# Six places for projection weights, latents scaled ahead of the low-half search, and sliding attention's keys ahead of its values

## The chip, the cores and the metric

The kernel runs on one core of a Trainium2 chip. The time is the device time of one execution in microseconds (us); shown is the median of several runs. A profile comes from one execution of its own. The engines are called as in the profile: PE (TensorE, matrix multiplications and transposes), PEld (its weight loads), DVE (VectorE), ACT (ScalarE), POOL (GpSimd) and SP (SyncE, which issues most DMAs). Each engine works through its own queue in order, and waits at an instruction whose inputs or target are not free.

## The reference

One decoder block over 1024 tokens and 16 learned meta tokens, all in float32:

```python
hn = rms_norm(h, attn_norm_g)
proj = hn @ w_in
aq, ak, av, bq, bkv, iq, ik, iw, gates = jnp.split(proj, IN_SPLITS, axis=-1)
o_a = sliding_window_sink_attention(aq, ak, av, sinks, bias_a)      # window 128, 8 heads, 2 key heads
q = (rms_norm(bq, q_norm_g) @ w_uq).reshape(b, p, 8, 64)
c_kv = rms_norm(bkv, kv_norm_g)                                     # latent keys/values, 128 wide
o_b = indexed_sparse_mla(q_abs, c_kv, iq, ik, iw, w_uv, bias_b)     # each query attends to its 256 best keys
mixed = sig(gA) * (o_a @ w_branch_a) + sig(gB) * (o_b @ w_branch_b)
h = h + mixed @ w_out
h = h + (silu(rms_norm(h) @ w_ffn_gate) * (rms_norm(h) @ w_ffn_up)) @ w_ffn_down
```

The 256 best keys of a query come from an index score, `sum over 4 heads of relu(iq . ik) * iw`; of equal scores the earlier keys count.

## The kernel before

The tokens lie in eight blocks of 128, and the meta tokens in a ninth of 16. Every float32 product is made of three: an operand is split into a high part (a copy rounded to `float32r`, made by ACT) and a low part (the difference, made by POOL or DVE), and `mm3` (L193 issues its matmuls) adds high x high, high x low and low x high. So each weight tile passes through a raw place filled by a DMA, a copy on ACT (L187, `wa_hi`) and a subtraction on POOL (L188, `wa_lo`).

`phase1` does, in this order of the program text:

- `load_x`, `setup`, `norm_x`: load the tokens, normalise and transpose them (`xt`, `xh`).
- `indexer`: the index projections and scores (`scores[j]`, for the blocks 1 to 7; block j has 144 + 128 j columns). The upper 16 bits of each score are kept as `high[j]`.
- `select_topk`: finds each row's 256th largest score bit by bit, first in the upper 16 bits, then in the lower ("low halves"). There are three searches side by side. `search_dve` handles the blocks 6, 4 and 1: in each of 16 steps DVE counts, for each block, the scores above a threshold (L815) and moves the threshold with three small operations (L819, L820; L832 to L834 in the low halves). `search_act` handles the blocks 7 and 2 in one group, 5 and 3 in another: ACT counts with a sign function and an accumulator (L857), and POOL moves the threshold (L865 once for each block of the group, then L866). Between the halves `low_halves` extracts the lower 16 bits (L801 on POOL) and blanks those whose upper half differs (L802 on DVE). Then DVE makes each block's mask: counts, equal scores, a running sum over them (L781 to L791), and POOL scales it (L792) and cuts it to the causal part (L538).
- `proj_tokens`: two projections of 256 columns each for all blocks. The first (`part` 0) gives the query latents. The second gives the 128 columns of the key latents and the 128 of sliding attention's values, which go to DRAM (L569). Squares are summed by ACT (L565); from them DVE makes `rlat`, the scale of every row.
- `window_inputs`: keys and queries of sliding attention, by feature, stored to DRAM (`wk_dram`, `wq_dram`).
- `latents`: DVE scales the latents (L586, `lraw`), PE transposes them (L198, tile `tp`), ACT and DVE split them into `qn` and `ck`.
- `sparse_inputs`: queries, keys and values of the sparse attention from the latents, stored to DRAM.
- `window_setup` and `window_block`: sliding attention. The biases are loaded and masked on POOL (L544, L545); the values are loaded into the one raw place `kraw` and split into `va` (L675 on ACT, L676 on POOL); the keys of the two key heads pass through the same raw place and are split in `stacked` into `ka` (L689 on ACT, L690 on DVE). Then follow sixteen blocks of scores, softmax and values.
- `gates`: the sigmoid gates, 672 matmuls that are issued here (the rest follows later). They are traced last, and each may run only after a given earlier matmul (`marks`), so they fill PE's gaps.

The text above is only an order of priority: a planner, `TileContext(nc, schedule_with_timeline_sim=True)`, puts every engine's queue in order by its own estimate of times, and places the waits. `tc.issue_after(i)` keeps the instructions of a block behind instruction `i` on its engine. A tile with a `tag` and `bufs` takes one of so many places, and a new one waits until the readers of the old one are done. The projection weights all go through `weights` with

```python
WA = dict(tag="wa", unit=512, bufs=4)
```

which means four high and four low places of 512 columns, while the raw parts pass through two places `wa_raw` in the pool `wg`. A projection of 256 columns needs four places, the keys' projection two.

## Time and profile before

| what | value |
|---|---|
| median of 3 runs | 1499.91 us (1499.42 to 1502.9) |
| profiled execution, its own time | 1500.29 us |
| its span, first to last instruction | 1498.5 us |
| granted PE clock, mean of the span | 0.969 |
| index projections and scores | to about 137 us of the span |
| projections, search, latents | about 137 to 356 us |
| sliding attention | about 384 to 480 us |
| sparse attention, gates' merge | about 480 to 745 us |
| output projection and feed-forward part | from about 748 us |

A row of the table by window gives, for a stretch of the span, its length, the busy time of each engine with the number of instructions, the share of the PE clock that was granted, the busy share of the DMA engines and GB/s. A row of the waits says which instruction waited for which, how long in total, how often, and the longest. A row of a timeline gives start, length, engine, line, operation, shapes and count; in brackets stands the engine's idle time just before it and who ended it. A row of the groups gives busy time and mean duration in ns. The chain of waits is followed back from the last instruction, and its rows give start, length and what was running.

### The profile page before, as it was taken

To read this page: it belongs to the slowest core of one execution; us is meant where nothing else is said; L and a number is where in the kernel's file an instruction comes from. 1 tells how busy PE (TensorE), PEld (TensorE's weight loads), DVE (VectorE), ACT (ScalarE), POOL (GpSimd) and SP (SyncE) were. 2 spreads that over 40 slices of the span, in tenths; PEclk is the share of its full clock that TensorE was granted. 3 is DMA by queue.
4 is the path that set the end of the run, shared out by engine and by line. 5 is a ranking of instruction groups with operands and counts; after the bars stand their busy time and mean duration, and the time that the engine had idled before them with its cause. 6 is when DMAs were issued, how large, how long until landed. Compare 5 with 4: busy or idle time off the path is not lost.

```text
span 1498.5 us, 21232 instructions
## 1 busy us (share of the span) xinstructions
PE 1388.4 (93%) x6847; PEld 1157.7 (77%) x6847; DVE 990.8 (66%) x2122; ACT 818.1 (55%) x1743; POOL 648.8 (43%) x823
## 2 busy tenths in 40 slices
PE   4999787999799799999899699999999999999997
PEld 3988785777587688888687478888888888888886
DVE  6258998036576787777697995444544447696585
ACT  5347684994688677886335643333333333444473
POOL 4137465666666557675300015555555555000004
PEclk9999888999899899999999899999999999999999
DMA  6421121246443845335931133332333338832332
GB/s 202 142 68 39 29 65 43 87 135 209 112 140 105 212 133 173 119 117 179 308 138 57 56 112 102 103 109 95 105 106 106 106 102 292 323 99 98 117 109 113
DMA packets 148038, 189.79 MB, mean 127 GB/s; under 512 B 11331, under 2 KB 95126, under 8 KB 147670
## 3 DMA queue, kind: packets, MB, share of 16 engines
q1 hardware_dynamic: 147568, 188.28, 39.1%
q8 instruction: 54, 0.88, 0.3%
q14 instruction: 58, 0.48, 0.1%
q10 hardware_dynamic: 198, 0.14, 0.0%
q0 software_dynamic: 160, 0.01, 0.0%
HBM read 133.49 MB, written 58.03 MB: 128 GB/s over the span
## 4 chain that ended last, share of the span: by engine, by line
PE 64%; DVE 14%; issue 6%; ACT 6%; DMA 5%; POOL 5%; SPq 1%; POOLq 0%; ACTq 0%; DVEq 0%
PE ps L193 25%; PE s L193 23%; PE gps L193 7%; DVE mask L815 4%; ACT mask L857 2%; PE pv L1049 2%; PE s L1007 2%; PE tp L1038 2%; DMA ga<-gate_dram 1%; PE tp L198 1%; POOL y L1510 1%; PE pv L193 1%; DMA kraw<-bk_dram 1%; DMA wa_raw<-in_w_in 1%; DVE hb L1267 1%
## 5 line engine op out<-in xcount | busy, mean ns | idle before, releaser
L1360 POOL TENSOR_TENSOR fhl<-fr,fhl 128x512 fp32r<-128x512 f32 x60 | 97.5, 1645 | 223.0 <-ACT fhl L1359 223.0
L1360 POOL TENSOR_TENSOR fhl<-fs,fhl 128x512 fp32r<-128x512 f32 x80 | 106.5, 1355 | 106.8 <-ACT fhl L1359 106.8
L188 POOL TENSOR_TENSOR w_lo<-w_raw,w_hi 128x512 fp32r<-128x512 f32 x60 | 81.2, 1356 | 93.9 <-ACT w_hi L187 75.8
L193 PE MATMUL s<-ht,fhl 128*128 128x512 f32 x384 | 121.8, 393 | 0.0
L193 PE MATMUL ps<-ht,fhl 128*128 128x512 f32 x320 | 101.1, 392 | 0.0
L193 PE MATMUL gps<-oh,w_hi 128*128 128x512 f32 x232 | 94.2, 406 | 4.1 <-ACT gt L914 4.1
L857 ACT ACTIVATE mask<-high,smallg 128x784 bf16<-128x784 uint16 (+3 forms) x66 | 70.2, 1063 | 46.1 <-POOL smallg L866 28.4
L193 PE MATMUL gps<-ol,w_hi 128*128 128x512 f32 x232 | 92.7, 399 | 0.0
L193 PE MATMUL gps<-oh,w_lo 128*128 128x512 f32 x232 | 92.1, 397 | 0.0
L193 PE MATMUL s<-yhl,fhl 128*128 128x512 f32 x396 | 90.6, 389 | 0.0
L193 PE MATMUL ps<-yhl,fhl 128*128 128x512 f32 x396 | 90.2, 389 | 0.0
L1430 ACT CAST yhl<-wd 128x512 fp32r<-128x512 f32 x66 | 41.1, 622 | 89.9 <-PE ps L193 50.2
L193 PE MATMUL s<-h,fhl 128*128 128x512 f32 x272 | 87.7, 393 | 0.8 <-DVE hb L1267 0.5
L193 PE MATMUL ps<-h,fhl 128*128 128x512 f32 x256 | 82.9, 395 | 5.1 <-ACT h L1317 5.1
L133 DVE TENSOR_TENSOR ptl<-tp,pth 128x512 fp32r<-128x512 f32 (+2 forms) x112 | 70.9, 645 | 23.9 <-ACT pth L127 22.6
L193 PEld LDWEIGHTS s<-yhl,fhl 128*128 128x128 f32 x396 | 74.3, 188 | 15.5
L193 PEld LDWEIGHTS ps<-yhl,fhl 128*128 128x128 f32 x396 | 74.3, 188 | 15.4
L193 PEld LDWEIGHTS s<-ht,fhl 128*128 128x128 f32 x384 | 72.0, 188 | 17.2 <-ACT fhl L1359 0.7
L865 POOL TENSOR_SCALAR smallg<-smallg 128x1 f32<-128x1 f32 x128 | 58.9, 463 | 59.9 <-ACT mask L857 59.5
L1359 ACT CAST fhl<-fr 128x512 fp32r<-128x512 f32 x66 | 39.8, 619 | 76.6 <-issue 36.1
L1431 DVE TENSOR_TENSOR yhl<-wd,yhl 128x512 fp32r<-128x512 f32 x66 | 45.6, 691 | 50.2 <-ACT yhl L1430 50.2
L193 PE MATMUL s<-lt,fhl 128*128 128x512 f32 x192 | 75.3, 392 | 0.0
(479 smaller groups left out, 4267.5 us busy)
## 6 DMA issues: line engine op xcount, KB each, us to landing
fr<-in_w_ffn_gate SPq DMA_DIRECT2D x22, 512.0 KB, 4.0
fr<-in_w_ffn_up SPq DMA_DIRECT2D x22, 512.0 KB, 4.5
wd<-in_w_ffn_down SPq DMA_DIRECT2D x44, 256.0 KB, 5.1
da<-acts SPq DMA_DIRECT2D x44, 256.0 KB, 3.6
w_raw<-in_w_in SPq DMA_DIRECT2D x40, 256.0 KB, 3.0
act<-a SPq DMA_DIRECT2D x33, 256.0 KB, 2.1
da<-act SPq DMA_DIRECT2D x33, 256.0 KB, 4.3
acts<-s SPq DMA_DIRECT2D x33, 256.0 KB, 2.0
```

Source lines behind the costliest of these rows:

```text
L133: nc.vector.tensor_sub(lo, ps, hi.bitcast(F32))
L188: (nc.vector if lo_dve else nc.gpsimd).tensor_sub(t[1], t[2], t[0].bitcast(F32))
L193: mm = self.nc.tensor.matmul(*args, **kw)
L815: nc.vector.tensor_scalar(self.mask[j], src[j], at[:, i:i + 1], None, op0=op, op1=ALU.add, accum_out=out[:, i:i + 1])
L857: nc.scalar.activation(self.mask[j], src[j], AF.Sign, bias=at[:, i:i + 1], scale=scale, accum_out=out[:, i:i + 1])
L865: g.tensor_scalar(c[:, o], acc[:, o], bar[:, o], b[:, o], op0=ALU.is_ge, op1=ALU.subtract)
L1007: nc.tensor.matmul(ps[:, :n], q[k][:, h, qc:qc + P], kb[:, h, at:at + n], start=k == 0, stop=k == 1)
L1038: mm = nc.tensor.transpose(pt[:, P * i:P * i + P], prs[par, e][:, NM + P * rr:NM + P * rr + P], self.ident)
L1359: nc.scalar.copy(hi, a[name])
L1360: (nc.gpsimd if q else nc.vector).tensor_sub(lo, a[name], hi.bitcast(F32))
L1430: nc.scalar.copy(hi, src)
L1431: nc.vector.tensor_sub(lo, src, hi.bitcast(F32))
```

## The change

- `WA` has six places instead of four, and its pool is opened after the indexer, in the room that this leaves.
- The weights of the first projection no longer lie there: `latent_weights` puts them into the two tiles that later hold `qn`, which move out of the pool `lt` into a pool of their own.
- `select_topk` becomes a generator. It issues the sixteen steps of all three searches in the upper halves, stops, and goes on after `proj_tokens`. `proj_tokens` now ends with the scaling of the latents. DVE's part of the lower halves is held behind the last of these scalings (`issue_after(self.scaled)`); the rest of the search follows.
- In `window_setup` the first head's keys are loaded and split before the values, the second head's after them; the meta tokens' values come before the others. The low part of the values, and of the very first queries, is made by DVE instead of POOL.
- In the search on ACT, the step on POOL becomes four operations on all blocks of a group at once, of which the first doesn't need the count; two other operations, the `is_lt` that prepares the keys and the scaling of the finished masks, move from POOL to DVE.
- The values' copy in `proj_tokens` becomes a ring of three tiles, the ring `st` of results on their way to DRAM has four places instead of five, and `stacked` takes its number of raw places as an argument, which is 1 everywhere.

```diff
-WA = dict(tag="wa", unit=512, bufs=4)
+WA = dict(tag="wa", unit=512, bufs=6)
...
-        wa = self.wa_es = ExitStack()
-        self.wp = wa.enter_context(self.pool("wa"))
         with self.pool("x") as xp, self.pool("setup") as tmp:
...
-        self.wq0 = self.weights(self.wp, raw_pool=self.wg, src=self.win(768, 256), **WA)
+        wa = self.wa_es = ExitStack()
+        self.qnp = wa.enter_context(self.pool("qn"))
+        self.wq0 = self.latent_weights()
         with self.pool("idx") as ip:
             self.indexer(ip)
+        self.wp = wa.enter_context(self.pool("wa"))
         self.spread_bias()
         n1 = len(self.tensor_insts)
-        self.select_topk(tk)
+        search = self.select_topk(tk)
+        next(search)
         with self.pool("lt") as lp:
             self.proj_tokens(lp)
+            next(search, None)
             self.window_inputs(lp)
...
+    def latent_weights(self):
+
+        nc, src = self.nc, self.win(768, 256)
+        parts = [self.qnp.tile([P, 2, T], F32R, name=f"wq{k}", tag=f"qn{k}", bufs=1).rearrange("p a (k n) -> p (a k) n", n=256)
+                 for k in range(2)]
+        for k in range(0, KC, 2):
+            raw = self.wg.tile([P, 512], F32, name="wa_raw", tag="wa_raw", bufs=2).rearrange("p (k n) -> p k n", k=2)
+            nc.sync.dma_start(raw, src[:, k:k + 2, :])
+            hi, lo = [t[:, k:k + 2] for t in parts]
+            nc.scalar.copy(hi, raw)
+            nc.gpsimd.tensor_sub(lo, raw, hi.bitcast(F32))
+        return [(parts[0][:, k], parts[1][:, k]) for k in range(KC)]
...
-                    nc.scalar.copy(vraw[:n, b], ps[:n, :P])
-                    nc.sync.dma_start(self.wv_dram[:n, b], vraw[:n, b])
+                    vraw = lp.tile([P, P], F32, name="vraw", tag="vraw", bufs=3)
+                    nc.scalar.copy(vraw[:n], ps[:n, :P])
+                    nc.sync.dma_start(self.wv_dram[:n, b], vraw[:n])
...
-        self.rlat = self.rsqrt(lp, ss, 2 * NBP, "rlat")
+        rlat = self.rsqrt(lp, ss, 2 * NBP, "rlat")
+        for b in [NB] + list(range(NB)):
+            n = NM if b == NB else P
+            for part, cc in list(enumerate((slice(0, 256), slice(256, 384))))[b // NB:]:
+                r = rlat[:n, part * NBP + b:part * NBP + b + 1]
+                self.scaled = nc.vector.tensor_scalar(self.lraw[:n, b, cc], self.lraw[:n, b, cc], r, None, op0=ALU.mult).ins
...
-            for b in bs:
-                for part, cc in list(enumerate((slice(0, 256), slice(256, 384))))[c0 // 2:]:
-                    r = self.rlat[:n, part * (NB + 1) + b:part * (NB + 1) + b + 1]
-                    nc.vector.tensor_scalar(raw[:n, b, cc], raw[:n, b, cc], r, None, op0=ALU.mult)
...
-        t = lp.tile([P, 512], F32, name="st", tag="st", bufs=5)[:n, :m]
+        t = lp.tile([P, 512], F32, name="st", tag="st", bufs=4)[:n, :m]
...
+        self.ka = [ap.tile([P, C], F32R, name=f"ka{g}") for g in range(2)]
+        self.stacked(ap, self.ka[0], self.wk_dram[:64])
         va = self.va = ap.tile([P, NBP, 2, 2, 64], F32R, name="va")
...
-        for n, bs in ((P, slice(0, NB)), (NM, slice(NB, NBP))):
+        for n, bs in ((NM, slice(NB, NBP)), (P, slice(0, NB))):
...
-            nc.gpsimd.tensor_sub(va[:n, bs, :, 1, :], raw[:n, bs], va[:n, bs, :, 0, :].bitcast(F32))
-        self.ka = [ap.tile([P, C], F32R, name=f"ka{g}") for g in range(2)]
-        for g in range(2):
-            self.stacked(ap, self.ka[g], self.wk_dram[64 * g:64 * g + 64])
+            nc.vector.tensor_sub(va[:n, bs, :, 1, :], raw[:n, bs], va[:n, bs, :, 0, :].bitcast(F32))
+        self.stacked(ap, self.ka[1], self.wk_dram[64:])
...
-        nc.gpsimd.tensor_sub(lo[:64], raw[:64], hi[:64].bitcast(F32))
+        (nc.gpsimd if g + u else nc.vector).tensor_sub(lo[:64], raw[:64], hi[:64].bitcast(F32))
...
         searches.append(self.search_dve(ap, DVE_ROWS, thr[:, :nd]))
+        for _ in range(16):
+            for s in searches:
+                next(s)
+        yield
+        with self.tc.issue_after(self.scaled):
+            next(searches[-1])
         while searches:
             searches = [s for s in searches if next(s, None) is not None]
...
-            nc.gpsimd.tensor_scalar(self.mask[j], eq[:, :W], -1.0, -NEG, op0=ALU.add, op1=ALU.mult)
+            nc.vector.tensor_scalar(self.mask[j], eq[:, :W], -1.0, -NEG, op0=ALU.add, op1=ALU.mult)
...
-            g.tensor_scalar(t, key, 0.0, 32767.0, op0=ALU.is_lt, op1=ALU.mult)
+            nc.vector.tensor_scalar(t, key, 0.0, 32767.0, op0=ALU.is_lt, op1=ALU.mult)
...
-                for i in range(n):
-                    o = slice(i, i + 1)
-                    g.tensor_scalar(c[:, o], acc[:, o], bar[:, o], b[:, o], op0=ALU.is_ge, op1=ALU.subtract)
-                g.tensor_scalar(b, c, -2.0 if k else -1.0, 1.0, op0=ALU.mult, op1=ALU.add)
+                m = 2.0 if k else 1.0
+                g.tensor_scalar(T1, b, m, 1.0, op0=ALU.mult, op1=ALU.add)
+                g.tensor_sub(c, acc, bar)
+                g.tensor_scalar(c, c, 0.0, -m, op0=ALU.is_ge, op1=ALU.mult)
+                g.tensor_add(b, T1, c)
...
-            self.stacked(kvp, kb[:, e], self.bk_dram[pr][64 * e:64 * e + 64])
+            self.stacked(kvp, kb[:, e], self.bk_dram[pr][64 * e:64 * e + 64], 1)
```

More of the change, by code (lines that the diff above doesn't have):

```diff
@@ L551, in proj_tokens @@
         self.lraw = lp.tile([P, NBP, 384], F32, name="lraw")
-        vraw = lp.tile([P, NBP, P], F32, name="vraw")
         junk = lp.tile([P, 256], F32, name="junk")
@@ L682, in window_setup, with stacked @@
             self.clear_lo(t)
-    def stacked(self, pool, dst, src):
+    def stacked(self, pool, dst, src, bufs=1):
         nc = self.nc
-        raw = pool.tile([P, (NB + 1) * P], F32, name="kraw", tag="kraw", bufs=1)[:, :C]
+        raw = pool.tile([P, (NB + 1) * P], F32, name="kraw", tag="kraw", bufs=bufs)[:, :C]
         self.doubled(raw, src)
```

2 lines of the change are left out of this document (1 added, 1 removed).

## Prediction, made before any run of the changed kernel

> **What bounds the kernel now.** I read the page first: TensorE (PE) is busy for 93% of the span, so a gain has to come from the places where it idles or runs at a reduced clock.
>
> ```profile
> span 1498.5 us, 21232 instructions
> PE 1388.4 (93%) x6847; PEld 1157.7 (77%) x6847; DVE 990.8 (66%) x2122; ACT 818.1 (55%) x1743; POOL 648.8 (43%) x823
> ```
>
> The change touches what lies between the index scores and the end of the sliding attention, about 137 to 480 us. I cut that stretch where the chain of waits changes its work, and asked for the table by window (columns: length, busy time of PE, PEld, DVE, ACT, POOL, then the granted PE clock).
>
> ```profile
> 137.00:160.00 23.00, 23.00 (x195) 22.95 (x194) 22.34 (x62) 16.41 (x47) 12.85 (x24) 1.00 0.00 1
> 160.00:218.00 58.00, 44.33 (x268) 40.07 (x268) 54.35 (x150) 41.82 (x121) 30.40 (x68) 0.82 0.17 46
> 218.00:244.00 26.00, 16.09 (x93) 13.86 (x91) 25.29 (x86) 11.57 (x30) 11.34 (x24) 0.85 0.20 57
> 244.00:303.00 59.00, 53.68 (x224) 42.38 (x224) 16.77 (x34) 50.89 (x116) 43.85 (x85) 0.93 0.27 83
> 303.00:356.00 53.00, 52.95 (x236) 43.88 (x235) 27.27 (x43) 41.06 (x90) 29.74 (x55) 0.95 0.49 162
> 356.00:384.00 28.00, 19.72 (x85) 15.42 (x83) 10.15 (x10) 8.38 (x14) 25.98 (x25) 0.92 0.60 176
> 384.00:480.00 96.00, 89.55 (x469) 73.37 (x470) 72.46 (x236) 79.39 (x227) 63.07 (x88) 0.95 0.41 115
> ```
>
> Length minus PE's busy time is PE's idle time: 13.7 us in 160:218, 9.9 in 218:244, 5.3 in 244:303, 0.1, 8.3, 6.5. Beside it a reduced clock stretches the matmuls; missing clock times busy time estimates that at 0.18 x 44.3 = 8.0 us, 0.15 x 16.1 = 2.4, 0.07 x 53.7 = 3.8, 2.6, 1.6 and 4.5. From 160 to 384 that is 37.3 us idle and 18.4 us slow: about 55 us is the most that any reordering here can bring. PE's own waits, longest first, name who ended the idle time:
>
> ```profile
> PE tp L198 <- DVE lraw L586: 9.9, 1, 9.9
> PE s L193 <- POOL wa_lo L188: 8.8, 4, 7.6
> PE s L193 <- DVE ka L690: 7.6, 1, 7.6
> PE s L193 <- ACT wa_hi L187: 6.1, 2, 3.8
> PE s L193 <- ACT vraw L568: 1.8, 1, 1.8
> ```
>
> These are exactly three places: projection weights (`wa`), scaled latents (`lraw`), and the first keys of sliding attention (`ka`).
>
> **Part 1: six places and a home of its own for the first weights.** The first projection's weights fill all four `wa` places; the second projection's can be split only when the first projection's last block has read them.
>
> ```profile
> 166.38 2.13 SPq L185 DMA_DIRECT2D wa_raw<-in_w_in  x4
> 184.61 4.12 POOL L801 TENSOR_SCALAR mask<-sc,smalld 128x912 uint16<-128x912 uint16 x3 [10.85 <-DVE smalld L823]
> 188.92 0.95 ACT L857 ACTIVATE mask<-high,smallg 128x784 bf16<-128x784 int16 x1 [11.59 <-POOL smallg L866]
> L188 POOL TENSOR_TENSOR wa_lo<-wa_raw,wa_hi 128x512 fp32r<-128x512 f32 x18 | 24.8, 1385 | 1.2 <-ACT wa_hi L187 1.2
> ```
>
> So the loads resume at 166.4. Worse, POOL, which makes `wa_lo`, stands for 10.85 us at L801, the low halves of VectorE's (DVE) rows, because DVE's search had not got that far; ACT's search stands 11.59 us behind POOL. PE's waits of 3.8 and 7.6 us follow. Afterwards the first weights lie in `qn`, all four tiles of the second projection fit at once, and the 23 us in which PE runs the first projection (137:160) cover their four splits (1.4 us each on POOL by the L188 row, 5.5 together). The two remaining places take the key weights. L801 is issued after the scaling of the latents, which needs the second projection's results, so it can no longer stand ahead of the weights that PE wants next. The loads themselves are as many as before. I take the 13.7 us idle and 8.0 us slow, less the 1.8 us for `vraw` (ACT) and 1 us for the remaining hand-overs: **19 us**.
>
> The Trainium skill, "TensorE: Matmul & The Clock Gate", section "What's actually happening", says that the clock falls to half after an idle window of about 3.4 us and returns after about as long a busy one. By it two stalls cost an estimated 2 x 1.7 = 3.4 us instead of 8.0, and the forecast below would be 4.6 us later. The clock of 0.82 in 160:218 is lower than that, and I keep the row.
>
> **Part 2: latents scaled ahead of the low-half search.** The scaling stands in DVE's queue behind the search:
>
> ```profile
> L586 DVE TENSOR_SCALAR lraw<-lraw,rlat_y x17: 268/333/1379, 243.1 to 248.0; 128x256 f32<-128x256 f32 x8, 128x128 f32<-128x128 f32 x8, 16x128 f32<-16x128 f32 x1
> 238.80 0.95 ACT L857 ACTIVATE mask<-high,smallg 128x784 bf16<-128x784 uint16 x1 [14.05 <-DVE smalld L832]
> 338.63 0.17 DVE L889 TENSOR_SCALAR smallg<-smallg 128x2 int32<-128x2 f32 x1 [8.48 <-POOL smallg L865]
> ```
>
> The 17 operations take 5 us. With part 1 the second projection ends near 218 - 13.7 - 8.0 = 196 us, plus small square roots and those 5 us: done near 204, before the keys' projection ends, and PE's 9.9 us are gone. DVE's low search starts near 204 instead of 186 and so ends near 261 instead of 243. Nothing waits for it there: the joint end of the search waits for ScalarE's (ACT) rows until 338.6, 77 us of cover. If that cover were gone, its 18 us would count in full. Behind the new wait stand the rest of DVE's bits, and, through L801, whatever POOL has queued next: splits of the query weights and ACT's search steps. Today's L801 row bounds that at 10.85 us; the keys' projection (most of PE's 16.1 busy us in 218:244 today) lies beside it, so I count nothing for it here beyond the charge in part 4. But ACT stood still as well, 14.05 us until 238.8, for low halves that DVE had queued behind its own bits; some of that may come back. Of 9.9 + 2.4 + 3.8 us I take **12 us**.
>
> **Part 3: the start of sliding attention.** Today the values come first, and they hold the only raw place. From the chain of waits (start, length, what):
>
> ```profile
> 372.17 1.51 POOL va L676
> 377.40 4.17 DMA kraw<-wk_dram
> 381.65 1.07 ACT ka L689
> 382.74 1.25 DVE ka L690
> ```
>
> The masks ahead of it, by groups and by the timeline:
>
> ```profile
> L792 POOL TENSOR_SCALAR mask<-mask 128x656 bf16<-128x656 bf16 x1 | 1.6, 1608 | 0.1
> 358.58 2.89 DVE L791 SCALAR_TENSOR_TENSOR mask<-sc,small,mask 128x400 bf16<-128x400 f32 x2
> 342.77 0.42 DVE L788 TENSOR_SCALAR mask<-sc,small 128x400 bf16<-128x400 f32 x1
> ```
>
> POOL is 26.0 of 28.0 us busy here, with masks (seven of L792), then bias masks, then `va`; the key load waits for `va`. Keys first removes the dependence on `va`; the load can go out at the latents' end near 357 and be landed 4 us later. What is late next is DVE: its mask work runs to 361.5, seven mask conversions come on top (one tensor and a constant take 0.42 us in L788, two tensors 1.45 in L791: 2.9 to 10 us, and I take 5, nearer to L788, which has the same operands), then `ka` at 1.25. The first scores could start near 368, if the search ends where it does now, and earlier if it ends earlier. But PE fills the time to 376 with gate matmuls, which it must then do later, so only its idle 7.6 us and some clock are to be had. The moved `va` and first query subtractions add about three 1.2 us operations to DVE (by `ka`). I take **5 us**.
>
> **Part 4: small things and new costs.** Four `is_lt` operations move from POOL to DVE, and the search's step on POOL becomes four operations instead of three, three of them behind the last count:
>
> ```profile
> L849 POOL TENSOR_SCALAR mask<-high 128x1040 int16<-128x1040 int16 x1 | 3.8, 3772 | 0.1
> L865 POOL TENSOR_SCALAR smallg<-smallg 128x1 f32<-128x1 f32 x126 | 58.1, 465 | 59.9 <-ACT mask L857 59.5
> L866 POOL TENSOR_SCALAR smallg<-smallg 128x2 f32<-128x2 f32 x64 | 13.2, 207 | 4.9
> L885 POOL TENSOR_TENSOR smallg<-smallg 128x2 f32<-128x2 f32 x1 | 0.2, 194 | 0.1
> 257.78 0.36 POOL L865 TENSOR_SCALAR smallg<-smallg 128x1 f32<-128x1 f32 x1 [0.21 <-ACT mask L857]
> 250.33 6.00 POOL L865 TENSOR_SCALAR smallg<-smallg 128x1 f32<-128x1 f32 x2
> ```
>
> Behind the last count stood one L865 and one L866, 0.36 (its undisturbed time, at 257.8) + 0.21; now three operations of 0.19 to 0.21 by L866 and L885, or 0.47 each by L865's mean. That is +0.03 to +0.84 us a step; I take the near row, +0.03, nothing over 33 steps of a group. The is_lt operations free some 12 us of POOL ahead of the search; I count nothing, since PE does not wait there. `vraw` in a ring of three makes ACT wait for the third store back; each block gives it about 4 us (36 us for nine), so three blocks cover about 12. Four `st` places instead of five cost nothing while SP isn't held. The explicit `1` for raw places changes nothing.
>
> One row is a warning: two L865 that take 0.72 us took 6.00 at 250.3, while DVE ran its masks, and the change gives DVE more such work. I charge **5 us**, the excess of that row once, also for ACT, whose 50.9 of 59 us in 244:303 leave little room to follow a faster PE. The Trainium skill, "SBUF — State Buffer", section "Who interferes with whom", gives a reason: GpSimd and some VectorE operations share a port pair, and the later one blocks for the whole instruction; the row agrees. By that rule each moved operation would hold POOL up, an estimated 5 us more at the scaling burst, which the keys' projection covers.
>
> **Sum.** 19 + 12 + 5 - 5 = 31 us. The profiled execution took 1500.3 us by itself (span 1498.5 and 1.8 around it), 0.4 above the median of 1499.9. Forecast: 1500.3 - 31 = **1469 us**.
>
> **Rivals.** (a) *The stall moves behind.* If ACT's search ends at 338.6 as now, because POOL or ACT again stand in queue order, what PE saves before 300 us is given back in front of the window blocks: they start near 368 instead of 384, and all that remains is 16 us: 1484. For it: ACT is busy for 92 of the 112 us in 244:356. Against it: its idle 11.6 and 14.05 us are of the kind that is removed. (b) *Slower: the search becomes the gate.* If the three dependent POOL operations cost 0.47 each and more under DVE's work, the end of the search slips by 33 x 0.84 = 28 us, the blocks start near 396, and the time is 1512. It decides from 16 us of slip on, 0.5 us a step. Against it: L866 and L885 at 0.2. (c) *The places don't help*, since the two raw tiles are the real limit: SP stays blocked behind them, and a smaller gain at the keys alone is eaten by the 5 us: 1500. Against it: 23 us of cover for four loads. (d) *Everything goes*, idle and slow: 1500.3 - 55 = 1446.
>
> **How the numbers follow.** Forecast 0.55 (its terms at half and at full: 1455 to 1483), (a) 0.19, (b) 0.10, (c) 0.08, (d) 0.08. About 0.3% is what a measurement of this kernel tells from no change, 4.5 us. Faster: 0.55 + 0.19 + 0.08 = 0.82; same: 0.08; slower: 0.10. The range leaves out (b) and most of (d): from 1448, nearly all that is to be had, to 1502, which takes in (c); about 0.16 is left outside.
>
> **What would show it.** Right: no PE wait above 2 us for `wa_lo`, `wa_hi` or `lraw`; `wa_raw` loads of the second projection before 160; L586 before 210 and the low-half counts after it; L801 on POOL without a 10 us wait; keys' projection ending near 215; first `ka` scores before 365. Part 3 is wrong if PE still idles over 5 us ahead of the first scores with DVE masks as the releaser (then a); part 4 if L865's successors take over 0.5 us each (then b). The forecast is wrong if POOL or ACT stand still elsewhere for 10 us because an instruction for the low halves heads the queue too early.

## The result and the profile after

| | before | after |
|---|---|---|
| median, us (5 runs each) | 1499.91 (1499.42 to 1502.94) | 1486.77 (1482.89 to 1487.61) |
| ratio | 1 | 0.9901, 95% interval 0.9886 to 0.9916 |
| profiled execution: span, us | 1498.5 | 1480.7 |

Faster by 1.0%, 13.1 us by the medians; the forecast was 31. The profiled execution of the changed kernel was the fastest of its five, so the two profiles lie 17.8 us apart, more than the medians. Beside the experiments below the kernel before took 1503 to 1504 us, and the changed kernel, run twice more, stood at 0.9875 (0.9854 to 0.9896) and 0.9868 (0.9847 to 0.989). The runs are therefore compared by their ratio to the kernel before that ran with them on the same chip, and between chips no closer than some 0.3%.

The page of the changed kernel:

```profile
span 1480.7 us, 21298 instructions
PE 1380.9 (93%) x6847; PEld 1149.3 (78%) x6847; DVE 1002.8 (68%) x2136; ACT 817.0 (55%) x1743; POOL 609.9 (41%) x873
```

Of the changed kernel, three rows of the window table with the prediction's cuts (length, busy PE, PEld, DVE, ACT, POOL, then granted clock):

```profile
160.00:218.00 58.00, 58.00 (x385) 52.60 (x384) 46.77 (x133) 48.72 (x141) 36.43 (x99) 1.00 0.24 69
218.00:244.00 26.00, 26.00 (x115) 21.15 (x114) 24.88 (x73) 18.48 (x44) 14.70 (x47) 1.00 0.24 83
244.00:303.00 59.00, 37.17 (x162) 29.30 (x161) 38.82 (x93) 48.99 (x109) 26.38 (x90) 0.80 0.20 67
```

The idle time that the change aimed at is gone: PE is busy in all of 160:244, at the full clock, where it had 23.6 us idle. But 244:303, with 5.3 us idle and a clock of 0.93 before, now has 21.8 us idle and 0.80. PE's two longest waits in this stretch of the changed kernel name what ended it; no wait for `wa_lo`, `wa_hi` or `lraw` is left:

```profile
PE s L193 <- ACT qn L129: 13.4, 1, 13.4
PE tp L198 <- DVE ck L135: 6.9, 1, 6.9
```

The timelines of the engines in the changed kernel tell why (start, length, instruction, idle time ahead of it and releaser). The new line numbers: L593 is the scaling of the latents, L825 VectorE's preparation of low halves, L838 its count, L880 ScalarE's count, L129 and L135 the high and low parts of the latents.

```profile
197.93 5.73 DVE L593 TENSOR_SCALAR lraw<-lraw,rlat_y 16x128 f32<-16x128 f32 x17
...
244.25 1.16 DVE L838 TENSOR_SCALAR_CACHE_REDUCE mask<-high,smalld 128x912 bf16<-128x912 uint16 x1
...
245.34 1.30 DVE L825 SCALAR_TENSOR_TENSOR high<-high,smallg,mask 128x1040 uint16<-128x1040 int16 x1
...
246.73 1.16 ACT L880 ACTIVATE mask<-high,smallg 128x1040 bf16<-128x1040 uint16 x1 [10.26 <-DVE high L825]
...
261.64 0.68 ACT L129 ACTIVATE qn<-tp,vec 128x512 fp32r<-128x512 f32 x1
...
262.37 0.80 PE L193 MATMUL s<-qn,wa_hi 128*128 128x512 f32 x1 [13.40 <-ACT qn L129]
270.02 2.25 PE L198 MATMUL tp<-ident,lraw 128*128 128x128 f32 x8 [6.86 <-DVE ck L135]
```

The latents are scaled by 203.7, as forecast, and PE transposes the first ones at 245.6, no earlier than in the kernel before (243.4). What it gained it spent on the keys' and queries' projections: their last matmul runs at 245.3, in the kernel before at 294.7. So none of that work is left to fill a stall behind 245, and DVE is counting its own low bits there. L825, which ScalarE's search needs, stands among them and comes at 245.3. ScalarE stands for 10.3 us, then works off what has piled up, so that the latents' high parts come at 261.6. Their low parts on DVE come when the last of its bits is done, after 265.

The gain can be booked from the index scores' end to the end of the gate matmuls, cut at the first scores of sliding attention and the first of sparse attention. Of the kernel before, and then of the kernel after, the table by these windows:

```profile
137.40:384.00 246.60, 209.37 (x1091) 178.21 (x1090) 155.79 (x378) 169.84 (x411) 153.84 (x275) 0.91 0.30 92
384.00:498.50 114.50, 104.13 (x528) 84.60 (x529) 82.13 (x254) 89.55 (x245) 71.05 (x98) 0.95 0.47 130
498.50:742.10 243.60, 230.62 (x1402) 201.52 (x1401) 184.39 (x519) 170.94 (x372) 146.38 (x229) 0.98 0.56 169
```

```profile
138.10:350.70 212.60, 189.77 (x1051) 163.00 (x1050) 163.85 (x391) 163.51 (x398) 116.28 (x312) 0.94 0.31 96
350.70:475.40 124.70, 111.32 (x568) 88.79 (x568) 83.36 (x255) 92.53 (x250) 79.91 (x107) 0.98 0.47 134
475.40:724.10 248.70, 233.78 (x1401) 203.13 (x1402) 185.25 (x520) 171.06 (x372) 143.63 (x230) 0.97 0.55 167
```

The stretch ahead of the first scores is 34.0 us shorter, the next is 10.2 longer and the last 5.1 longer: 18.7 us are left. Part of the 34 was only put off. 40 matmuls fewer run ahead of the first scores (1091 to 1051) and exactly 40 more behind them (528 to 568), since filling matmuls have slid. PE's idle time fell by 14.4 us in the first stretch (37.2 to 22.8) and rose by 3.0 (10.4 to 13.4) and 1.9 (13.0 to 14.9) in the others: 9.5 us less in all. The rest of the 18.7 us, 9.2, is PE's busy time, 534.9 us in place of 544.1 for as many matmuls; the clock is higher in the first two stretches (0.91 to 0.94, 0.95 to 0.98) and slightly lower in the third.

### The profile page after: what moved, and what is told of

It reads as the page before. It is cut to its first block, busy times and chain, and to the rows that moved or that the text cites. A ratio compares the mean times of both kernels' runs of the same rounds, so it can differ in the third digit from the quotient of the medians.

```text
span 1480.7 us, 21298 instructions
## 1 busy us (share of the span) xinstructions
PE 1380.9 (93%) x6847; PEld 1149.3 (78%) x6847; DVE 1002.8 (68%) x2136; ACT 817.0 (55%) x1743; POOL 609.9 (41%) x873
## 4 chain that ended last, share of the span: by engine, by line
PE 69%; DVE 14%; DMA 5%; issue 4%; ACT 3%; POOL 3%; SPq 1%; POOLq 0%; DVEq 0%; ACTq 0%
PE ps L193 28%; PE s L193 25%; PE gps L193 9%; DVE mask L838 3%; PE pv L1073 2%; DMA kraw<-bk_dram 1%; PE s L1031 1%; PE tp L1062 1%; PE tp L198 1%; POOL y L1534 1%; DVE ptl L133 1%; DVE pb L1035 1%; PE pv L193 1%; DMA ga<-gate_dram 1%; DVE hb L1291 1%
## 5 line engine op out<-in xcount | busy, mean ns | idle before, releaser
L193 PEld LDWEIGHTS s<-yhl,fhl 128*128 128x128 f32 x396 | 74.3, 188 | 15.5
L193 PEld LDWEIGHTS ps<-yhl,fhl 128*128 128x128 f32 x396 | 74.3, 188 | 15.5
L880 ACT ACTIVATE mask<-high,smallg 128x1040 bf16<-128x1040 int16 (+3 forms) x66 | 70.7, 1071 | 24.0 <-DVE high L825 13.3
L1383 ACT CAST fhl<-fs 128x512 fp32r<-128x512 f32 x88 | 54.6, 625 | 33.1 <-PE s L193 17.4
```

The costliest lines, as they stand in the source:

```text
L193: mm = self.nc.tensor.matmul(*args, **kw)
L880: nc.scalar.activation(self.mask[j], src[j], AF.Sign, bias=at[:, i:i + 1], scale=scale, accum_out=out[:, i:i + 1])
L1383: nc.scalar.copy(hi, a[name])
```

## The experiments

Two theories at first. **Theory 1**: VectorE's low-half search, held back to where the latents come, stands in VectorE's queue ahead of what ScalarE and TensorE want. **Theory 2**: ScalarE's own load delays the latents, wherever VectorE's search is put. Two more came up on the way: that the selection of the keys (searches, then masks on VectorE) bounds the stretch whatever TensorE waits for ahead of it; and that part 4, charged as a cost, is where the gain comes from.

| run | ratio to before | 95% interval |
|---|---|---|
| e1, places only | 1.0023 | 1.001 to 1.0036 |
| e2, no hold | 0.9912 | 0.9892 to 0.9931 |
| e3, low search behind the latents | 0.9943 | 0.9926 to 0.9959 |
| e4, values first | 0.9857 | 0.9833 to 0.988 |
| the changed kernel again | 0.9875 | 0.9854 to 0.9896 |
| and beside e8 | 0.9868 | 0.9847 to 0.989 |
| e5, search cut 8 + 8 | 0.9854 | 0.983 to 0.9878 |
| e6, e5 with values first | 0.9837 | 0.9815 to 0.9858 |
| e7, part 4 undone | 0.9945 | 0.9925 to 0.9964 |
| e8, search cut 12 + 4, values first | 0.9792 | 0.9773 to 0.9811 |
| e8 again | 0.9826 | 0.9807 to 0.9845 |
| e9, only the step of part 4 undone | 0.9823 | 0.9804 to 0.9841 |
| e10, part 4 alone | 0.991 | 0.9891 to 0.993 |
| e12, e5 without ties | 0.9776 | 0.9757 to 0.9794 |
| e13, e9 with is_lt on GpSimd | 0.9925 | 0.9906 to 0.9944 |
| e14, e9 with masks on GpSimd | 0.9853 | 0.9832 to 0.9873 |
| e15, e8 with the old step | 0.9832 | 0.981 to 0.9854 |
| e16, part 4 without its step | 0.9915 | 0.9894 to 0.9935 |

**e1: part 1 alone.**

```diff
 # in the kernel before
-WA = dict(tag="wa", unit=512, bufs=4)
+WA = dict(tag="wa", unit=512, bufs=6)
-        self.wq0 = self.weights(self.wp, raw_pool=self.wg, src=self.win(768, 256), **WA)
+        self.wq0 = self.latent_weights()
... and the rest of part 1
```

> The kernel before with part 1 alone: six places for projection weights, the first weights in the places of qn, a ring of three for the stores of the values. The scaling of the latents stays where it was, behind VectorE's search of the low halves. Theory 1 (the low-half search of VectorE stands in its queue ahead of what TensorE wants next, wherever it is put): the waits for wa_lo and wa_hi go, the second projection ends some 15 to 20 us earlier, but the scaling cannot start before VectorE's low search has ended near 243, so the wait for lraw grows from 9.9 to about 25 us and little is left: 1494 to 1500. The forecast's sum, part 1 by itself: 19 us, 1481. If the places do not help at all, the waits for wa_lo stay at 7 us or more and the time is 1500.

Measured 1.0023, slightly slower, and outside all three expectations. PE's longest waits in this run:

```profile
PE s L193 <- ACT wa_hi L187: 12.1, 1, 12.1
PE s L193 <- DVE ka L704: 11.3, 1, 11.3
PE tp L198 <- DVE ck L135: 7.8, 1, 7.8
PE ps L193 <- ACT vraw L582: 6.5, 1, 6.5
```

The waits moved: for `wa_hi` one of 12.1 us in place of 3.8, for `vraw` 6.5 in place of 1.8, for the low part of `ck` 7.8, a wait not among the five of before, and for `ka` 11.3 in place of 7.6. By itself part 1 is worth nothing. That the wait for `lraw` would grow, as theory 1 had it, did not happen: the planner put the scaling between two bits.

**e2: the hold removed.**

```diff
 # in the changed kernel
-        with self.tc.issue_after(self.scaled):
-            next(searches[-1])
```

> The changed kernel without the one line that holds VectorE's low-half search back until the latents are scaled: the search again starts when its high halves are done, near 190. Theory 1: the scaling comes after the search, near 245 instead of 198, TensorE has its long wait ahead of the latents for lraw instead of for qn and ck, and the time is 1485 to 1495, because the hold only moved the wait. The forecast's term for this part, 12 us: 1499. Rival theory 2 (ScalarE's own load between 160 and 300 is what delays the latents' high parts, VectorE's queue is not): no change, 1487 within 3.

Measured 0.9912, within theory 1's range, and 0.1 to 0.4% behind the changed kernel (0.9901, 0.9875 and 0.9868 in its three measurements, on other chips). By these figures the hold is worth 2 to 7 us, little more than half at most of the 12 that were counted for its part; two of the three intervals overlap with that of e2, so even this is not clear of noise. The waits are not the ones of theory 1: none is for `lraw`, the longest are 12.3 us for `vraw`, 9.9 for the low part of `ck` and 7.9 for `wa_hi`.

**e3: the low search behind the latents.**

```diff
 # in the changed kernel: self.scaled becomes the latents' last L135
-            nc.vector.scalar_tensor_tensor(lo, ps, scale, hi.bitcast(F32), op0=ALU.mult, op1=ALU.subtract)
+            self.scaled = nc.vector.scalar_tensor_tensor(lo, ps, scale, hi.bitcast(F32), op0=ALU.mult, op1=ALU.subtract).ins
...
             self.latents(lp)
+            next(search, None)
...
+        acts = searches[:-1]
+        while acts:
+            acts = [s for s in acts if next(s, None) is not None]
+        yield
         with self.tc.issue_after(self.scaled):
             next(searches[-1])
...
```

> The changed kernel with VectorE's low-half search held back further: behind the last split of the latents instead of behind their scaling. The low halves for ScalarE's rows stay ahead. Theory 1: VectorE prepares ScalarE's low halves as soon as the high halves are done, so ScalarE's stand of 10.3 us goes; the latents' low parts no longer queue behind VectorE's bits; TensorE's 13.4 and 6.9 us ahead of the latents shrink below 5 us together, the first matmul of qn comes near 248 instead of 262, and the time falls by 8 to 18 us: 1469 to 1479. VectorE's search then starts near 255 and ends near 310, still ahead of ScalarE's. Rival theory 2 (ScalarE's own load is the bound): the wait for the latents' high parts stays at 10 us or more, 1485 to 1490. Rival theory 3: VectorE's search, ended 45 us later, now delays the masks and so the first scores: 1490 or more.

The first scores in this run, then rows of its tables by windows:

```profile
347.62 0.68 PE L193 MATMUL s<-ka,qhi 128*128 128x144 f32 x2 [13.41 <-DVE ka L708]
```

```profile
218.00:244.00 26.00, 26.00 (x114) 21.21 (x113) 3.00 (x2) 24.15 (x56) 17.08 (x54) 1.00 0.31 94
...
140.30:347.60 207.30, 187.11 (x1043) 160.21 (x1042) 133.70 (x341) 162.56 (x395) 112.89 (x309) 0.97 0.32 99
347.60:489.10 141.50, 115.63 (x577) 94.29 (x578) 114.60 (x306) 92.86 (x251) 78.63 (x109) 0.90 0.44 120
```

The waits of 13.4 and 6.9 us are gone (2.4 and 2.0 us remain), so VectorE's queue was their cause, and theory 2 falls. But theory 1's time fails too: 0.9943, worse than the changed kernel. VectorE was busy for only 3.0 of the 26 us in 218:244, finished its search 87 us later (351.5 against 264.6), with the low part of `ka` among its last counts, and the masks behind it held up the sliding attention, in which PE has 25.9 us idle in place of 13.4. It is theory 3's case: the later search delays what comes behind it.

**e4 and e6: values ahead of keys again.** The kernel before's order in `window_setup`, in the changed kernel (e4) and in e5 (e6).

> The changed kernel with part 3 undone: sliding attention's values ahead of its keys, their subtractions on GpSimd as before. By the forecast's term of 5 us: 1492. If keys first is worth nothing here, because the search's end and the masks set the first scores: 1487 within 3. If its benefit is larger, since the search now ends 18 us earlier and GpSimd's masks and values would stand ahead of the keys' load: 1495, with TensorE waiting 10 us or more for ka.

> The search cut in two as in the run before it, and the values ahead of the keys as in the kernel before. If keys first is worth nothing to the end, because gate matmuls fill TensorE ahead of the first scores in either order: within 3 us of the cut search alone. If keys first costs something later: 4 us faster than that. By the forecast's term: 5 us slower.

> The changed kernel itself once more, as the measure for the runs beside it on the same chip. 0.990 of the kernel before, as measured first; on this chip the kernel with the values first stood at 0.986, so a ratio near 0.986 here would say that the order of keys and values is worth nothing, and one near 0.990 that keys first costs about 5 us.

e4 stands at 0.9857 against 0.9868 to 0.9901 for the changed kernel, e6 at 0.9837 against 0.9854 for e5. Undoing part 3 costs nothing and may gain 2 or 3 us; the intervals overlap, so no gain from that order is shown. A gain of 5 us by keys first is excluded. The first stretch of e4:

```profile
138.30:362.20 223.90, 199.75 (x1091) 171.02 (x1090) 163.22 (x390) 166.49 (x402) 129.96 (x321) 0.95 0.32 99
```

With keys first the first scores come 11.5 us earlier (350.7 against 362.2), but with 40 matmuls fewer done ahead of them (1051 against 1091).

**e5: the search cut in two.**

```diff
 # in e3, with the latents' last L135 now kept as self.low_part and self.scaled the last scaling again:
 # eight bits behind the scaling, the rest behind the low parts
-        yield
         with self.tc.issue_after(self.scaled):
             next(searches[-1])
+        for _ in range(7):
+            next(searches[-1])
+        yield
+        with self.tc.issue_after(self.low_part):
+            next(searches[-1])
```

> The changed kernel with VectorE's low-half search cut in two: eight bits behind the scaling, in the time in which VectorE stood idle in the run with the whole search behind the latents (205 to 245), and eight bits behind the last split of the latents. Theory 1 (what limits the change is where VectorE's low bits stand in its queue): the long waits for the latents' parts (13.4 and 6.9 us) fall below 6 us together, as with the whole search behind them, and VectorE's search ends near 305 instead of 351, beside ScalarE's, so that masks and first scores no longer give it back: 1468 to 1476. Theory 4 (the lead is lost in front of the first scores in any case, because the masks' 26 us behind the search bound them): 1483 to 1490.

The first scores in this run, and the first row of its table by windows:

```profile
347.12 0.68 PE L193 MATMUL s<-ka,qhi 128*128 128x144 f32 x2 [11.19 <-DVE ka L708]
...
139.50:347.10 207.60, 187.61 (x1041) 161.06 (x1040) 161.57 (x390) 161.91 (x396) 117.44 (x312) 0.95 0.33 99
```

0.9854, the time of theory 4, against 0.9875 for the changed kernel on the same chip, with intervals that overlap. The stall ahead of the latents falls from 20.3 us to 8.1 (5.6 and 2.5 for the two parts of `ck`), the search ends at 308, and still the first scores start at 347.1, 3.6 us earlier than in the changed kernel: PE waits 11.2 us for `ka`, whose low part stands behind the masks on DVE. This points to the selection as a second bound, and to the stall ahead of the latents as time that PE would largely have waited in any case.

**e12: the selection shortened.** e5 leaving out the ranking of equal scores, 14 operations of DVE behind the search.

```diff
 # in e5
-            nc.vector.tensor_tensor_scan(rank[:, :W], eq[:, :W], eq[:, :W], 0.0, op0=ALU.add, op1=ALU.max)
-            nc.vector.scalar_tensor_tensor(eq[:, :W], rank[:, :W], col(cnt, j), eq[:, :W], op0=ALU.is_le, op1=ALU.mult)
```

> The run with the search cut in two, keys first, leaving out the ranking of equal scores in the selection (the running sum and the comparison with the rank, 14 operations of VectorE, some 18 us behind the search); all keys that equal the threshold stay in. If the selection's end gates the first scores there: masks done near 326 instead of 344, TensorE's wait of 11.2 us for ka gone, first scores near 333 instead of 347, and the time 6 to 11 us below the cut search, 0.978 to 0.981. If the first scores wait for something else: 0.985 within 0.002.

The last mask and the first scores in this run's timeline, then the first row of its table by windows:

```profile
320.08 0.60 DVE L822 TENSOR_SCALAR mask<-mask 128x400 bf16<-128x400 bf16 x2
...
342.06 0.34 PE L193 MATMUL s<-ka,qhi 128*128 128x144 f32 x2
```

```profile
138.90:342.10 203.20, 191.52 (x1052) 164.52 (x1051) 141.40 (x377) 162.79 (x398) 115.06 (x314) 0.97 0.34 102
```

0.9776, 0.8% below e5, about 12 us for 20 us less work of VectorE in this stretch (161.6 to 141.4). The two ran on different chips, but the intervals are well apart: the selection's end did hold the first scores up. PE no longer waits for `ka`, and its idle time ahead of the first scores is 11.7 us in place of the 20.0 of e5 (207.6 long, 187.6 busy). The next bound is close behind: the masks end 27 us earlier than in e5, the first scores come only 5 us earlier, not 14 as expected, since ScalarE's copy of the keys now waits for their load until 338.4. This isn't a version to use, since all keys that equal the threshold stay in.

**e8: twelve bits ahead, four behind.** With the values first, and four bits placed by hand behind the low halves of ScalarE's rows, in the 14 us in which DVE stood idle in e5.

```diff
 # in e6, behind the first eight bits
+        with self.tc.issue_after(self.low_ins[2]):   # L825 of ScalarE's last row
+            next(searches[-1])
+        for _ in range(3):
+            next(searches[-1])
         yield
```

> The run with the search cut in two and the values first, with four more of VectorE's bits in the 14 us that it stood idle there (241 to 256, behind the low halves of ScalarE's rows and ahead of the latents' low parts). If the selection of the sparse keys (searches, then masks on VectorE) is what the first scores wait for once the latents no longer stall: VectorE's search ends near 291 instead of 307, the masks near 332 instead of 342, TensorE's idle time ahead of the first scores falls by 5 us or more, and the time by 3 to 8 us, to 0.979 to 0.982 of the kernel before. If not: 0.984 within 0.002.

```profile
138.10:347.00 208.90, 197.30 (x1081) 169.05 (x1079) 162.59 (x390) 164.86 (x401) 130.10 (x320) 0.98 0.34 104
347.00:465.00 118.00, 105.14 (x538) 84.80 (x538) 83.19 (x252) 90.48 (x247) 73.88 (x102) 0.97 0.48 132
465.00:713.10 248.10, 233.97 (x1402) 203.43 (x1402) 184.29 (x520) 170.95 (x372) 144.41 (x230) 0.97 0.56 167
```

0.9792, median 1473.06 us: the fastest kernel with the whole computation. PE has 11.6 us idle ahead of the first scores, at a clock of 0.98, with 30 matmuls more done there than in the changed kernel. It was then run again, beside the changed kernel on one chip:

> The changed kernel a third time, beside the fastest version on one chip. Its two ratios so far are 0.9901 and 0.9875, from two chips: 0.987 to 0.991.

> The fastest version (twelve bits ahead of the latents' low parts and four behind them, values first) again, beside the changed kernel on one chip. If its lead of 0.8%, so far taken from ratios of two chips, is its own: 0.979 to 0.982, with the changed kernel 0.6% or more behind. If the lead was one of the chips: within 0.4% of the changed kernel.

Here it stands at 0.9826 (median 1476.47 us) and the changed kernel at 0.9868 (1483.21 us). The intervals stay apart, if narrowly, so it beats both kernels, but the lead over the changed one is 0.4% here, between the two expectations, not 0.8%. How much of it the four placed bits bring beyond e6 (0.9837) is not settled. The gain over the kernel before is 26 to 31 us.

**e7, e9, e10, e16: part 4 undone, in part and alone.** e7 puts back all of it in the changed kernel, e9 only the step of the search; e10 makes part 4 alone in the kernel before, e16 that without the step.

```diff
 # e7, in the changed kernel; e9 is the last hunk alone
-            nc.vector.tensor_scalar(self.mask[j], eq[:, :W], -1.0, -NEG, op0=ALU.add, op1=ALU.mult)
+            nc.gpsimd.tensor_scalar(self.mask[j], eq[:, :W], -1.0, -NEG, op0=ALU.add, op1=ALU.mult)
-            nc.vector.tensor_scalar(t, key, 0.0, 32767.0, op0=ALU.is_lt, op1=ALU.mult)
+            g.tensor_scalar(t, key, 0.0, 32767.0, op0=ALU.is_lt, op1=ALU.mult)
-                m = 2.0 if k else 1.0
...
-                g.tensor_add(b, T1, c)
+                for i in range(n):
+                    o = slice(i, i + 1)
+                    g.tensor_scalar(c[:, o], acc[:, o], bar[:, o], b[:, o], op0=ALU.is_ge, op1=ALU.subtract)
+                g.tensor_scalar(b, c, -2.0 if k else -1.0, 1.0, op0=ALU.mult, op1=ALU.add)
```

> The changed kernel with part 4's moves undone: the search's step on GpSimd as it was (an operation for each row and one for the group), the last mask operation and the is_lt operations back on GpSimd. The forecast charged part 4 with 5 us, so by it this run is 5 us faster, 1482. Rival: the moves are worth something, because ScalarE's search waits for GpSimd in each of its 33 steps and the run without the hold, which has them, was 16 us faster than the run with the places alone, which has not: 8 to 12 us slower, 1495 to 1499, with ScalarE's search ending near 330 instead of 320.

> The changed kernel with only the search's step on GpSimd as it was before (an operation for each row, then one for the group; two dependent operations behind the last count instead of three); the is_lt and mask operations stay on VectorE. All three undone together cost 10 us (0.9945 against 0.9875). If the step carries that: 0.992 or more. If the moved operations carry it: 0.9875 within 0.002. By the forecast's charge for the step, next to nothing (0.03 us a step), the second.

> The kernel before with part 4's moves alone: four operations instead of three in the search's step on GpSimd, is_lt and the last mask operation on VectorE. The forecast charged the part with 5 us: 1.003. If the moves shorten the selection, which ends in front of the first scores: 0.993 to 0.996, with ScalarE's search ending some 8 us before 338 and TensorE's wait for the first ka shorter. If they are worth something only together with the other parts: 1.000 within 0.002.

> The kernel before with nothing but the is_lt and the last mask operations on VectorE. With the step's change beside them it stood at 0.991. If the step costs something of its own: 0.986 to 0.988, as much as the whole change, or more. If the step is free in that order of work: 0.991 within 0.002.

e7 is 0.7% slower than the changed kernel on the same chip, 10 us, where the forecast had it 5 us faster. The path is not the one expected: ScalarE's search ends at 322.1, not near 330, and the first scores come at 351.0 against 352.1. What is missing is work done by then. The stretch ahead of the first scores in e7, and in the changed kernel beside it:

```profile
138.10:351.04 212.94, 182.37 (x1002) 154.15 (x1000) 158.18 (x380) 163.46 (x399) 128.88 (x257) 0.95 0.30 91
```

```profile
138.10:352.08 213.98, 191.10 (x1055) 164.15 (x1054) 162.03 (x393) 164.06 (x400) 115.63 (x312) 0.94 0.32 96
```

In e7 PE has done 53 matmuls fewer and has stood 30.6 us in place of 22.9, among others 3.8 us for `wa_hi` and 1.9 for `lraw`, both from ScalarE, waits that the other run doesn't have.

e10, the kernel before with these small moves alone, stands at 0.991: they gain 13 us without any of parts 1 to 3, as much as the whole change in its first measurement. Its first stretch, up to the first scores:

```profile
138.50:371.60 233.10, 204.59 (x1090) 173.72 (x1089) 153.77 (x389) 166.87 (x405) 129.38 (x323) 0.93 0.32 97
```

It is 13.5 us shorter than in the kernel before, with as many matmuls done (1090 and 1091), and ScalarE's search ends 10 us earlier (328.1 against 338.1). Here the gain lies wholly ahead of the first scores, beside a selection that ends earlier.

The step is the exception. Undone in the changed kernel (e9) it gains some 0.5%; in the kernel before it is worth nothing (e16, 0.9915 against 0.991). In e9 PE still stands 20.9 us for the low part of `ck`, as long as in the changed kernel, and yet e9 is among the faster runs: one more sign that this stall isn't what sets the time.

**e13, e14, e15: which of the moves, and the step again.** e13 is e9 with the `is_lt` operations on POOL, e14 is e9 with the last mask operations on POOL, e15 is e8 with the old step.

> The run with the search's step as before (0.9823), with the four is_lt operations ahead of the search back on GpSimd as well; the last mask operations stay on VectorE. The prediction counted nothing for them, because TensorE does not wait there. If these 12 us of GpSimd ahead of the search were on the path of the selection all the same: ScalarE's first counts come some 9 us later, its search ends near 325 instead of 316, and the ratio is 0.988 to 0.994. If the mask operations carry the difference between 0.9823 and 0.9945: 0.9825 within 0.002.

> The run with the search's step as before (0.9823), with the seven last mask operations back on GpSimd; the is_lt operations stay on VectorE. The prediction put them on VectorE's path at 5 us, as a cost of having moved them. If that is right: 0.979. If on GpSimd, 1.2 to 1.6 us each by the rows of the kernel before, ahead of the bias masks, they hold up the first scores: 0.985 to 0.990, with the first scores some 8 us later.

> The fastest run so far (twelve bits of VectorE ahead of the latents' low parts and four behind them, values first, 0.9792), with the search's step on GpSimd as it was. If the step's cost is one of its own, in each of the 33 steps: its 8 us come off here as well, 0.974. If it came from VectorE's instructions for ScalarE's low halves landing late in the queue, which this version places by hand: 0.979 within 0.002.

The `is_lt` operations in e9 and then in e13 (the source line's answer: count, shortest, median and longest in ns, first and last start), each with ScalarE's first count of its longest row and the window 137:160:

```profile
L872 DVE TENSOR_SCALAR mask<-high x2: 431/935/1439, 123.9 to 146.2; 128x784 int16<-128x784 int16 x1, 128x1040 int16<-128x1040 int16 x1
...
148.49 1.16 ACT L880 ACTIVATE mask<-high,smallg 128x1040 bf16<-128x1040 int16 x1 [1.84 <-DVE small L843]
...
137.00:160.00 23.00, 23.00 (x196) 22.91 (x194) 22.53 (x54) 19.40 (x54) 16.27 (x30) 1.00 0.19 46
```

```profile
L872 POOL TENSOR_SCALAR mask<-high x2: 3764/3768/3772, 124.4 to 147.8; 128x784 int16<-128x784 int16 x1, 128x1040 int16<-128x1040 int16 x1
...
158.31 1.16 ACT L880 ACTIVATE mask<-high,smallg 128x1040 bf16<-128x1040 int16 x1 [6.25 <-DVE high L874]
...
137.00:160.00 23.00, 22.73 (x193) 22.53 (x191) 22.40 (x56) 12.79 (x36) 15.09 (x18) 1.00 0.18 46
```

0.9925 against 0.9823: the four `is_lt` operations carry about 15 us, give or take the 4 or 5 that two chips can differ by. On POOL the one for 1040 columns starts at 147.8 and takes 3.77 us, and DVE's next operation on its result (L874) comes only at 157.6, behind two more rounds of DVE's own counts; the longest row's search starts at 158.3 in place of 148.5, and ScalarE, which stands at that count, leaves its other group too: it is busy for 12.8 of the 23 us in place of 19.4. The masks then end some 11 us later, as the last long mask operation in e9 and in e13 shows:

```profile
337.22 1.32 DVE L814 SCALAR_TENSOR_TENSOR mask<-sc,small,mask 128x1040 bf16<-128x1040 f32 x1
```

```profile
348.64 1.32 DVE L814 SCALAR_TENSOR_TENSOR mask<-sc,small,mask 128x1040 bf16<-128x1040 f32 x1
```

The first scores come 5.2 us later in e13 (356.7 against 351.5), with 43 matmuls fewer done (1021 against 1064). So what the four operations cost is shown; how much of it goes by the selection's end, and how much by ScalarE's other work, which PE waits for as in e7, is not.

e14 is 0.3% behind e9, some 4 us, with intervals that just overlap: the mask operations carry little, and not the loss that was charged. e15 fell outside what was expected of it: the old step, 0.5% better in the changed kernel, is no better in e8 (0.9832 against 0.9792 and 0.9826). Its effect isn't one of the step itself, then; that the planner makes another order of work of it each time is the likely reason: PE stands 11.7 us for the low part of `ck` in e15, 5.6 in e8. Which instructions make the difference in e9 and in e15 was not traced further and stays open.

## What the prediction had right, and where it failed

- **Direction and range** held; the forecast of 1469 us was 18 us too low, because 13 of the 31 us came. That the direction held is in part luck: beside e7, on one chip, the changed kernel gained 18.8 us by its ratio, and 10 of them came from part 4, which was booked as a loss.
- **The step that failed** is the one that makes PE's idle time into a gain: "about 55 us is the most that any reordering here can bring", and from it 19 + 12 + 5 = 36 us for parts 1 to 3. Together they are worth 8 us (e7, 0.9945). The sum took PE's waits ahead of the first scores for the bound of the stretch, and put the chain beside them, from the searches over the masks to `ka`, at nothing. When most of the waits are removed (e3, e5), PE waits for `ka` instead, 13.4 and 11.2 us, because VectorE comes to the low part of `ka` only behind its bits or its masks; when the selection is shortened as well (e12), the time falls. Rival (a) had this mechanism, and its 1484 us is 3 us from the median. It tied it to ScalarE's search ending at 338.6 and the first scores near 368, which came at 320.2 and 350.7, so that its number fits so well is luck.
- **The three places of PE's waits** were read rightly, and the waits went, down to 1.0 us for `ka`: L593 ran at 197.9 to 203.7 ("done near 204"), the low search from 211 to 265 ("near 204" to "near 261"), PE had no idle time to 244, the first scores came at 350.7 ("before 365").
- **Part 2 failed at "Nothing waits for it there".** The cover of 77 us was true for DVE's thresholds, but not for what stood behind DVE's bits in its queue: the preparation of ScalarE's low halves (ScalarE stood 10.26 us) and the low parts of the latents. TensorE paid with 20.3 us. The prediction did write down that ScalarE's stand "may come back", but priced it only as a part of the 5 us; and it looked for the sign in an instruction that heads the queue too early, where L825 came too late. e3 and e5 show the cause of the stall, and e5 that removing it alone gains little.
- **Part 1, 19 us:** alone it gave nothing (e1). Its idle time was real, but alone it moves to the next waits.
- **Part 3, 5 us:** nothing to be seen (e4, e6). The prediction had the reason, that gate matmuls fill PE until then and must be done later, and still took 5.
- **Part 4, a loss of 5 us, had the wrong sign.** The passage that failed reads: "The is_lt operations free some 12 us of POOL ahead of the search; I count nothing, since PE does not wait there." On VectorE they let the longest row's search start earlier (148.6 in the changed kernel, 154.4 in the kernel before), and they are worth about 15 us in e9's order of work (e13). By which path is open, as said above. The step of the search cost what was forecast for each operation (L888 at a median of 194 ns), but undone it gained some 8 us in one order of work and nothing to be seen in two others:

```profile
L888 POOL TENSOR_TENSOR smallg<-smallg x64: 187/194/1983, 127.1 to 320.3; 128x2 f32<-128x2 f32 x64
```

- One number of its working is slightly off: half of the 31 us would leave 1485, not 1483. Nothing hangs on it.
- Part 4 alone gives 13 us on its chip, the others without it 8 (e7), and all together 15, 19 and 20 by the three ratios: within what chips differ by, the two gains add. A better order (e8) reaches 26 to 31 us; that this is near the forecast's sum is a coincidence, since part 3 is undone in it. Idle time and missing clock times busy time ahead of the first scores, reckoned as in the prediction, come to 37.2 + 0.09 x 209.4 = 56.0 us before, 22.8 + 0.06 x 189.8 = 34.2 after and 11.6 + 0.02 x 197.3 = 15.5 in e8. The time fell by less each time.

## What to carry to other kernels

Before counting an engine's idle time as a gain, look for the chain that runs beside it to the same point; if it ends there too, or later, part of that idle time is only cover for it. Here going after the waits alone gave little (e1, e3, e5), the small moves that let the other chain end earlier gave 13 us by themselves (e10), and both together the most (e8); a small operation can be worth more than the waits that are easy to see. When work is held back on an engine that issues in order, list what stands behind it in that queue for other engines, and cut it so that a part fills the engine's idle time and the rest goes behind what is wanted. A lead at some point of the run is a gain only as far as the same work has been done by then: count the matmuls on both sides.

## What the runs showed of the hardware

- The same comparison on int16 takes 3.76 us for 784 columns and 3.77 us for 1040 on POOL (e13), and 1.44 us for 784 and 0.43 us for 1040 on DVE (e9; the L872 rows above). Why the shorter one took longer on DVE was not looked into.
- After PE's stalls, which begin at 249 in both runs, the clock stayed at half for some us after the work had come back. Of the changed kernel, and then of e8, by short windows, with the first matmul behind e8's stall:

```profile
249.00:252.00 3.00, 0.00 (x0) 0.00 (x0) 2.86 (x10) 2.72 (x9) 1.46 (x8) 1.00 0.23 87
252.00:255.00 3.00, 0.00 (x0) 0.00 (x0) 2.90 (x9) 3.00 (x9) 1.12 (x7) 0.58 0.00 0
...
274.00:276.00 2.00, 2.00 (x6) 1.51 (x6) 2.00 (x2) 1.84 (x5) 1.90 (x2) 0.50 0.01 4
276.00:278.00 2.00, 2.00 (x10) 1.58 (x8) 1.00 (x2) 1.70 (x4) 1.14 (x6) 0.90 0.00 0
```

```profile
254.54 1.12 PE L198 MATMUL tp<-ident,lraw 128*128 128x128 f32 x4 [5.56 <-DVE ck L135]
...
256.00:258.00 2.00, 2.00 (x8) 1.49 (x7) 0.00 (x0) 2.00 (x5) 1.31 (x4) 0.50 0.00 0
258.00:260.00 2.00, 2.00 (x7) 1.58 (x7) 0.10 (x1) 2.00 (x6) 1.72 (x6) 0.70 0.13 22
260.00:262.00 2.00, 2.00 (x10) 1.61 (x9) 1.30 (x2) 2.00 (x6) 0.34 (x2) 1.00 0.76 241
```

If the clock is either full or half within a window, the means of 0.58, 0.90 and 0.70 give the moments of change. It fell some 3.5 us into the stall. In e8, where PE worked again from 254.5, it was back at about 259.2, after 4.7 us; in the changed kernel, where PE worked again from 270.0, at about 276.4, after 6.4 us. The Trainium skill, "TensorE: Matmul & The Clock Gate", section "What's actually happening", has at least one window of about 3.4 us for both ways and says that the window runs freely; the fall agrees with it, and both returns took longer than one window and less than two.
